# Moving part of a norm phase's vector work to GpSimd, and the order of its start

## The chip, the cores and the metric

One core of a Trainium2 chip runs the whole kernel. The metric is device time in microseconds of one execution; lower is better. Engine names are the profile's: PE is TensorE (with PEld, its weight loads), DVE is VectorE, ACT is ScalarE, POOL is GpSimd, and SP issues most of the DMAs.

## The reference, cut to what matters

The program is one hybrid layer (attention and an mLSTM, both gated) on 256 tokens of width 1024, all float32. The change touches only its first phase: the modulated norm, and the projection of the normed tokens to queries and keys.

```python
ada = c @ w_ada + b_ada
shift, scale, gate = jnp.split(ada[:, None, :], 3, axis=-1)
h = _rmsnorm(x, norm_w) * (1 + scale) + shift
(qa, ka, va, za, qm, km, vm, zm, om, ig, fg, ga, gm) = jnp.split(h @ w_in, SPLIT_IDX, axis=-1)
```

`qa` and `ka` are the first 2048 columns of `h @ w_in`. Everything behind (the other projections, attention, mLSTM, output) is the same program text before and after.

## The kernel before, in words

Every product of the layer keeps close to float32 accuracy by splitting each operand into a high part (rounded to the matmul's format) and a low part (what is left), and adding three products: high by high, high by low, low by high. `hTh` and `hTl` are the two parts of the normed tokens, transposed; `wrh` and `wrl` are those of the weight rows of this phase.

The norm phase runs over eight contraction blocks k of 128 rows of `w_in`. In one block the kernel needs:

- two reductions over the row blocks of `w_ada` (tile `adat`) against the broadcast `c` (tile `cb`), which give the scale column `Ab` and the shift column `Bb` (`modulation` for block 0, `modulation_sum` behind, on DVE; the accumulator is read out by a second short instruction);
- `hTh` and `hf`, x's transposed block times `Ab` plus `Bb`, on ACT, and `hTl = hf - hTh` on DVE (`modulate`, `modulate_low`);
- the high part of 2048 weight columns by casts on ACT (`split_hi`), the low part by subtractions on DVE (`split_low`, line 192);
- 24 matmuls of 128x512 on PE (`mm_row`, line 202) into four accumulators `pm[0..3]`, one for each 512 columns.

Before block 0 x's sums of squares are taken, a power gives the reciprocal norm (`rstd`, on POOL), ACT scales an identity by it (`diag`), and PE multiplies x's blocks by that diagonal: this transposes and norms them at once (`x_transposes`, tile `xps`); copies bring the result from PSUM to `xnT`.

No scheduler decides the order: the engines take their instructions in the order in which the program text issues them. That order is written by hand in the string `P1_STEPS`. Each step is a letter and a block: `i`/`j` are hTh and hf, `U`, `z` the low parts of the first and second 512 columns, `v` that of the last 1024 (`g` and `h` are its halves), `G` is hTl, `c` and `k` the scale and shift reductions, `a` and `b` what ACT makes of them, `w`, `x`, `y` the high parts, `e` the block's matmuls, `R` the copies that lay out the relative bias (on POOL), `L` the next loads. `P1_LOADS` is the order of the DMAs on SP: `Ak1`/`Ak0` are the scale and shift rows of block k (512 KB each), `Wkp` the pieces of its weight rows. Behind the norm phase the next products begin with lines 1178 to 1180 (matmuls) and 519 (their weights' low parts).

Of the kernel before, what the change touches and what calls it, by code (L numbers as in the profile page):

```python
# [70 lines left out]
def tile_hybrid(ctx: ExitStack, tc: tile.TileContext, x, c, params2, w_row, w_va, ada_mod, ada_gate,  # L71
                w_in, w_att_proj, w_ml_proj, w_out, out):
    nc = tc.nc
# [67 lines left out]
    def load_row(k, piece):
        if k not in wrow:
            wrow[k] = rawp.tile([128, 2048], F32, name="raw", tag=f"raw{k % 6}", bufs=1)
        cs = slice(*W_PIECES[piece])
        nc.sync.dma_start(wrow[k][:, cs], w_row[k, :, cs])

    def modulation(k):

        kc = slice(k, k + 1)
        for s, m, b, r in ((1, prm[:, P_NW + k:P_NW + k + 1], b1[:, kc], Ab), (0, 1.0, prm[:, P_SH + k:P_SH + k + 1], Bb)):  # L150
            nc.vector.tensor_tensor_reduce(sq, adat[k][:, s], cb, m, b, OP.mult, OP.add, r[:, kc])
# [16 lines left out]
    def modulate(k, parts="ij"):  # L168
        kc = slice(k, k + 1)
        src = xnT[:, k] if k else xps[0][:, 0]  # L170
        if "i" in parts:
            nc.scalar.activation(hTh[:, k], src, AF.Identity, scale=Ab[:, kc], bias=Bb[:, kc])
# [3 lines left out]
        if k:
            nc.scalar.activation(hf[k], src, AF.Identity, scale=Ab[:, kc], bias=Bb[:, kc])
        else:
            nc.vector.tensor_scalar(hf[k], src, Ab[:, kc], Bb[:, kc], op0=OP.mult, op1=OP.add)

    def modulate_low(k):
        nc.vector.tensor_tensor(hTl[:, k], hf[k], hTh[:, k].bitcast(F32), op=OP.subtract)
# [1 line left out]
    def split_hi(k, c0, c1, copy=nc.scalar.copy):  # L184
        if k not in wsp:
            wsp[k] = (ph.tile([128, NR], F32R, name="wrh", bufs=3), ph.tile([128, NR], F32R, name="wrl", bufs=3))
        copy(wsp[k][0][:, c0:c1], wrow[k][:, c0:c1])  # L187

    def split_low(k, e, c0, c1):
        h, l = wsp[k]  # L190
        cs = slice(c0, c1)
        e.tensor_tensor(l[:, cs], wrow[k][:, cs], h[:, cs].bitcast(F32), op=OP.subtract)  # L192
# [24 lines left out]
    ssa = ph.tile([128, 8], F32, name="ssa")[:, 0:1]  # L217
    cb = ph.tile([128, D], F32, name="cb")

    def rstd(t):  # L220
        nc.gpsimd.tensor_tensor(rsx[:, t:t + 1], ssx[:, t:t + 1], mhalf[:, 0:1], op=OP.pow)


# [19 lines left out]
    nc.vector.tensor_tensor_reduce(sq, xt[:, 0], xt[:, 0], 1.0 / D, EPS, OP.mult, OP.add, ssx[:, 0:1])  # L243
    rstd(0)
    nc.scalar.activation(xnT[:, 4:6].rearrange("p k s -> p (k s)"), xt[:, 1, 0:512], AF.Square, scale=1.0 / 32, accum_out=ssa)
    nc.vector.tensor_tensor_reduce(sq[:, 512:D], xt[:, 1, 512:D], xt[:, 1, 512:D], 1.0 / D, EPS, OP.mult, OP.add, ssx[:, 1:2])
    nc.vector.tensor_tensor(ssx[:, 1:2], ssx[:, 1:2], ssa, op=OP.add)
# [77 lines left out]

# [929 lines left out]
```

## Time and profile before

| | before |
|---|---|
| median of 3 runs | 346.5 us (346.23 to 347.0) |
| the profiled execution | 346.51 us, span 344.5 us |
| busy in the span: PE, DVE, ACT, POOL | 339.0, 276.6, 228.7, 85.7 us |
| PE's clock as granted | 0.998 of full speed |
| HBM read over the span | 82.43 MB |

The page gives busy times by engine, a map of the span in 40 slices, the chain of work that ended last, and groups of instructions by line; the trace behind it gives each instruction's start and duration. A timeline row reads: start, duration, engine, line, operation, written tile <- read tiles, shapes, how many were merged into the row, and in brackets how long the engine had been idle and what it waited for. An instruction's duration can overlap its follower's by some 0.1 us, so what one costs in a row of many is read from start to start.

### The profile page before, as it was taken

To read this page: it belongs to the slowest core of one execution; us is meant where nothing else is said; L and a number is where in the kernel's file an instruction comes from. 1 tells how busy PE (TensorE), PEld (TensorE's weight loads), DVE (VectorE), ACT (ScalarE), POOL (GpSimd) and SP (SyncE) were. 2 spreads that over 40 slices of the span, in tenths; PEclk is the share of its full clock that TensorE was granted. 3 is DMA by queue.
4 is the path that set the end of the run, shared out by engine and by line. 5 is a ranking of instruction groups with operands and counts; after the bars stand their busy time and mean duration, and the time that the engine had idled before them with its cause. 6 is when DMAs were issued, how large, how long until landed. Compare 5 with 4: busy or idle time off the path is not lost.

```text
span 344.5 us, 6230 instructions
## 1 busy us (share of the span) xinstructions
PE 339.0 (98%) x2408; PEld 318.2 (92%) x2408; DVE 276.6 (80%) x420; ACT 228.7 (66%) x355; POOL 85.7 (25%) x83
## 2 busy tenths in 40 slices
PE   7999999999999999999999999999999999999996
PEld 7787889999999999999998888888989999999995
DVE  6999996979995979776997878897797677769952
ACT  4868779799787676766757577777666563735410
POOL 4700002843201836554131233422000102000000
PEclk9999999999999999999999999999999999999999
DMA  7999999989581496267797999999998038260011
GB/s 300 417 412 416 415 419 421 314 287 359 153 338 62 163 380 242 84 209 272 254 280 199 191 180 256 255 240 276 351 357 337 1 124 331 98 245 0 2 61 63
DMA packets 30909, 84.09 MB, mean 244 GB/s; under 512 B 3224, under 2 KB 5152, under 8 KB 30240
## 3 DMA queue, kind: packets, MB, share of 16 engines
q1 hardware_dynamic: 26376, 74.78, 57.8%
q0 software_dynamic: 4352, 8.39, 14.0%
...
q14 instruction: 10, 0.08, 0.1%
HBM read 82.43 MB, written 1.25 MB: 243 GB/s over the span
## 4 chain that ended last, share of the span: by engine, by line
PE 98%; ACT 1%; POOL 0%; DVE 0%; issue 0%; POOLq 0%
PE mm L1188 15%; PE mm L1185 15%; PE mm L1187 15%; PE pm L202 13%; PE mm L1178 4%; PE mm L1180 4%; PE mm L1179 4%; PE aux L1161 4%; PE aux L1162 4%; PE aux L1163 4%; PE mm L1171 3%; PE xps L267 1%; PE mm L1200 1%; PE aux L709 1%; PE mm L1199 1%; PE mm L1198 1%
## 5 line engine op out<-in xcount | busy, mean ns | idle before, releaser
L519 DVE TENSOR_TENSOR wl<-raw,wh 128x1024 fp32r<-128x1024 f32 (+1 forms) x104 | 126.3, 1228 | 34.3 <-ACT wh L515 33.4
L515 ACT CAST wh<-raw 128x1024 fp32r<-128x1024 f32 (+1 forms) x112 | 111.7, 1018 | 24.5 <-PE mm L1187 11.7
L1185 PE MATMUL mm<-hTh,wh 128*128 128x256 f32 x320 | 90.0, 281 | 0.0
L1187 PE MATMUL mm<-hTl,wh 128*128 128x256 f32 x320 | 88.8, 278 | 0.0
L1188 PE MATMUL mm<-hTh,wl 128*128 128x256 f32 x320 | 88.8, 278 | 0.0
L1187 PEld LDWEIGHTS mm<-hTl,wh 128*128 128x128 f32 x320 | 60.3, 189 | 0.2
L1185 PEld LDWEIGHTS mm<-hTh,wh 128*128 128x128 f32 x320 | 60.2, 188 | 0.2
L1188 PEld LDWEIGHTS mm<-hTh,wl 128*128 128x128 f32 x320 | 60.2, 188 | 0.0
L768 POOL DMA_DIRECT2D raw<-in_w_in_dram x16 | 19.5, 1222 | 49.3 <-DVE wl L519 38.3
L1178 PE MATMUL mm<-wh,hTh 128*128 128x344 f32 (+1 forms) x80 | 28.0, 350 | 0.0
L1180 PE MATMUL mm<-wh,hTl 128*128 128x344 f32 (+1 forms) x80 | 27.7, 346 | 0.0
L1179 PE MATMUL mm<-wl,hTh 128*128 128x344 f32 (+1 forms) x80 | 27.7, 346 | 0.0
L519 POOL TENSOR_TENSOR wl<-raw,wh 128x1024 fp32r<-128x1024 f32 x8 | 20.0, 2531 | 15.8 <-ACT wh L515 10.5
L187 ACT CAST wrh<-raw 128x512 fp32r<-128x512 f32 (+1 forms) x24 | 18.2, 761 | 7.6 <-DMA raw<-in_w_row_dram 7.6
L192 DVE TENSOR_TENSOR wrl<-raw,wrh 128x512 fp32r<-128x512 f32 (+1 forms) x26 | 20.5, 811 | 1.1 <-ACT wrh L187 1.1
L202 PE MATMUL pm<-wrh,hTh 128*128 128x512 f32 x64 | 19.8, 391 | 0.0
L202 PE MATMUL pm<-wrh,hTl 128*128 128x512 f32 x64 | 19.8, 391 | 0.0
L202 PE MATMUL pm<-wrl,hTh 128*128 128x512 f32 x64 | 19.1, 396 | 0.0
L1188 PE MATMUL mm<-yah,wl 128*128 128x256 f32 x64 | 17.7, 276 | 0.0
L1185 PE MATMUL mm<-ymh,wh 128*128 128x256 f32 x64 | 17.7, 276 | 0.0
L1185 PE MATMUL mm<-yah,wh 128*128 128x256 f32 x64 | 17.7, 276 | 0.0
L1187 PE MATMUL mm<-yal,wh 128*128 128x256 f32 x64 | 17.7, 276 | 0.0
(252 smaller groups left out, 774.0 us busy)
## 6 DMA issues: line engine op xcount, KB each, us to landing
...
```

The lines of the kernel that those rows point to most:

```text
L187: copy(wsp[k][0][:, c0:c1], wrow[k][:, c0:c1])
L192: e.tensor_tensor(l[:, cs], wrow[k][:, cs], h[:, cs].bitcast(F32), op=OP.subtract)
L202: nc.tensor.matmul(pm[ch][:, t], a[:, k, t * 128:(t + 1) * 128], b[:, cs], start=k == 0 and i == 0, stop=k == KT - 1 and i == 2)
L515: nc.scalar.copy(h, w)
L519: e.tensor_tensor(l, w, h.bitcast(F32), op=OP.subtract)
L768: nc.gpsimd.dma_start(rawt[li][:, ks], w_block(ch["name"], *BLOCK_SUMS[ch["product"]])[:, ks], accum_op=OP.add)
L1178: nc.tensor.matmul(o, a, wh[:, kk], start=first, stop=False)
L1179: nc.tensor.matmul(o, a, wl[:, kk], start=False, stop=False)
L1180: nc.tensor.matmul(o, b, wh[:, kk], start=False, stop=last)
L1185: nc.tensor.matmul(o, wh[:, kk, cs], sh_[:, k], start=first and i % 2 == 0, stop=False, skip_group_check=True)
L1187: nc.tensor.matmul(o, wh[:, kk, cs], sl_[:, k], start=False, stop=False, skip_group_check=True)
L1188: nc.tensor.matmul(o, wl[:, kk, cs], sh_[:, k], start=False, stop=last and i % 2 == 1, skip_group_check=True)
```

## The change: what it does

1. In every block the low part of the last 512 columns (1536 to 2047) is subtracted on POOL and no longer on DVE; DVE keeps 1024 to 1535. In block 0 both of these are on POOL, and so is one cast.
2. The statistics of x: the first tile is squared and summed in halves on DVE and ACT, the second wholly on ACT; POOL scales the first diagonal, ACT the second. The copies that bring `cb` from PSUM go from ACT to DVE.
3. Block 0's two modulation sums are taken in halves of 512, each half with its own DMA.
4. All transposes of x's first tile come ahead of those of the second. In block 0, hf goes from DVE to ACT, the first cast and the first copy of `xnT` from ACT to DVE.
5. Block 1's last weight piece is loaded ahead of block 2's scale rows. The relative-bias copies move from block 0 to the ends of blocks 1 and 2.

The core of the diff:

```diff
-P1_LOADS = ["A01 A00 W00 W01 A11 A10"] + [f"W{k}0 W{k}2 A{k + 1}1 W{k}3 A{k + 1}0" for k in range(1, 7)] + ["W70 W72 W73"]
+P1_LOADS = (["a01 b01 a00 b00 W00 W02 W03 A11 A10", "W10 W12 W13 A21 A20"]
+            + [f"W{k}0 W{k}2 A{k + 1}1 W{k}3 A{k + 1}0" for k in range(2, 7)] + ["W70 W72 W73"])
...
+        half = ph.tile([128, 2], F32, name="sums", bufs=2)
         for s, m, b, r in (...):
-            nc.vector.tensor_tensor_reduce(sq, adat[k][:, s], cb, m, b, OP.mult, OP.add, r[:, kc])
+            for cs, init, to in ((slice(0, D // 2), b, half[:, s:s + 1]), (slice(D // 2, D), half[:, s:s + 1], r[:, kc])):
+                nc.vector.tensor_tensor_reduce(sq[:, cs], adat[k][:, s, cs], cb[:, cs], m, init, OP.mult, OP.add, to)
...
+        if t:
+            nc.gpsimd.tensor_scalar(ssx[:, 1:2], ssa[:, 1:2], 1.0, EPS, op0=OP.mult, op1=OP.add)
+        else:
+            nc.vector.tensor_tensor(ssx[:, 0:1], ssx[:, 0:1], ssa[:, 0:1], op=OP.add)
         nc.gpsimd.tensor_tensor(rsx[:, t:t + 1], ssx[:, t:t + 1], mhalf[:, 0:1], op=OP.pow)
...
+    xsq = xnT[:, 4:8].rearrange("p k s -> p (k s)")
+    nc.vector.tensor_tensor_reduce(sq[:, 0:512], xt[:, 0, 0:512], xt[:, 0, 0:512], 1.0 / D, EPS, OP.mult, OP.add, ssx[:, 0:1])
+    nc.scalar.activation(xsq[:, 0:512], xt[:, 0, 512:D], AF.Square, scale=1.0 / 32, accum_out=ssa[:, 0:1])
+    rstd(0)
+    nc.gpsimd.tensor_scalar(diag[:, 0], ident, rsx[:, 0:1], None, op0=OP.mult)
     for n in range(2):
-        nc.scalar.copy(cb[:, n * 512:(n + 1) * 512], pc[:, n])
+        nc.vector.tensor_copy(cb[:, n * 512:(n + 1) * 512], pc[:, n])
+    nc.scalar.activation(xsq, xt[:, 1], AF.Square, scale=1.0 / 32, accum_out=ssa[:, 1:2])
     rstd(1)
+    nc.scalar.activation(diag[:, 1], ident, AF.Copy, scale=rsx[:, 1:2])
...
+                 w=lambda k: split_hi(k, 0, 512, nc.scalar.copy if k else nc.vector.tensor_copy), ...
+                 g=lambda k: split_low(k, nc.vector, 1024, 1536),
+                 h=lambda k: split_low(k, nc.gpsimd, 1536, NR), p=lambda k: split_low(k, nc.gpsimd, 1024, 1536),
+                 Y=lambda k: split_hi(k, 1024, 1536), Z=lambda k: split_hi(k, 1536, NR, nc.gpsimd.tensor_copy),
```

`P1_STEPS` is a table of steps, so its effect is shown as the order in which the engines then have their instructions. First DVE from block 3's hTl to block 4's, before (`adat`, `cb` are read by the reductions, called ISA here; `wrl` is a low part):

```order
L182 TENSOR_TENSOR hTl<-hf,hTh 128x256
L158 ISA sq,sums<-adat,cb 128x1024
L158 ISA sums 128x1
L192 TENSOR_TENSOR wrl<-raw,wrh 128x512
L158 ISA sq,sums<-adat,cb 128x1024
L158 ISA sums 128x1
L192 TENSOR_TENSOR wrl<-raw,wrh 128x1024
L192 TENSOR_TENSOR wrl<-raw,wrh 128x512
L182 TENSOR_TENSOR hTl<-hf,hTh 128x256
```

The same place of DVE in the changed program:

```order
L182 TENSOR_TENSOR hTl<-hf,hTh 128x256
L161 ISA sq,sums<-adat,cb 128x1024
L161 ISA sums 128x1
L192 TENSOR_TENSOR wrl<-raw,wrh 128x512
L161 ISA sq,sums<-adat,cb 128x1024
L161 ISA sums 128x1
L192 TENSOR_TENSOR wrl<-raw,wrh 128x512 x2
L182 TENSOR_TENSOR hTl<-hf,hTh 128x256
```

The subtraction of 1024 columns behind the second reduction has become one of 512; the order is otherwise the same.

POOL from the powers of the statistics on, before (`rvec` is the relative bias):

```order
L221 TENSOR_TENSOR rsx<-ssx,mhalf 128x1 x2
L291 COPY rvec<-xt 128x16
L296 COPY rvec<-xt 128x3
L296 COPY rvec<-xt 128x2
L296 COPY rvec<-xt 128x3 x2
```

POOL from the same place on, in the changed program, up to block 2's subtraction:

```order
L228 TENSOR_TENSOR rsx<-ssx,mhalf 128x1
L252 TENSOR_SCALAR diag<-ident,rsx 128x128
L225 TENSOR_SCALAR ssx<-ssa 128x1
L228 TENSOR_TENSOR rsx<-ssx,mhalf 128x1
L187 CAST wrh<-raw 128x512
L192 TENSOR_TENSOR wrl<-raw,wrh 128x512 x3
L299 COPY rvec<-xt 128x16
L304 COPY rvec<-xt 128x3
L304 COPY rvec<-xt 128x2
L304 COPY rvec<-xt 128x3 x2
L304 COPY rvec<-xt 128x4 x2
L304 COPY rvec<-xt 128x5
```

A scaling, a cast and three subtractions (two of block 0, one of block 1) now stand ahead of the bias copies, of which nine come before block 2's subtraction and eight before block 3's; those of blocks 4 to 7 follow with nothing between them.

More of the change, by code (lines that the diff above doesn't have):

```diff
@@ L35 @@
 P_CB, P_CW, P_ML, P_QN, P_KN, P_G, P_GT, NPRM2 = 0, 16, 80, 88, 89, 90, 91, 99
-P1_LOADS = ["A01 A00 W00 W01 A11 A10"] + [f"W{k}0 W{k}2 A{k + 1}1 W{k}3 A{k + 1}0" for k in range(1, 7)] + ["W70 W72 W73"]
-P1_STEPS = ("K5 D0 D1 D2 E0 E1 E2 T3 C0 w0 R0 R1 R2 R3 U0 H0 G0 x0 t0 B0 P0 z0 y0 t3 B2 t2 t1 B1 c1 a1 w1 k1 g0 h0 Q0 q0 n0 m0 "
+P1_LOADS = (["a01 b01 a00 b00 W00 W02 W03 A11 A10", "W10 W12 W13 A21 A20"]
+            + [f"W{k}0 W{k}2 A{k + 1}1 W{k}3 A{k + 1}0" for k in range(2, 7)] + ["W70 W72 W73"])
+P1_STEPS = ("K5 D0 D1 D2 D3 E0 E1 E2 E3 C0 H0 w0 U0 G0 t0 x0 B0 P0 z0 Z0 t3 Y0 B2 t1 t2 B1 p0 h0 c1 a1 w1 k1 Q0 q0 N0 M0 "
             + "".join(f"b{k} i{k} U{k} j{k} G{k} x{k} L1 c{k + 1} z{k} y{k} a{k + 1} "
-                      f"w{k + 1} " + (f"g{k} k{k + 1} h{k}" if k == 2 else f"k{k + 1} v{k}") + f" e{k} " for k in range(1, 7))
-            + "b7 i7 U7 j7 G7 x7 z7 y7 v7 P7 Q7 q7 N7 M7").split()
+                      f"w{k + 1} k{k + 1} g{k} h{k} {('R0 R1', 'R2 R3')[k - 1] if k < 3 else ''} e{k} " for k in range(1, 7))
+            + "b7 i7 U7 j7 G7 x7 z7 y7 g7 h7 P7 Q7 q7 N7 M7").split()
 WARM = 5
@@ L134, in tile_hybrid, with load_ada @@
     adat, wrow, wsp, hf = {}, {}, {}, {}
-    def load_ada(k, h):
+    def load_ada(k, h, c0=0, c1=D):
         if k not in adat:
             adat[k] = ph.tile([128, 2, D], F32, name="adat", bufs=4)
-        nc.sync.dma_start(adat[k][:, h], ada_mod[k, h])
+        nc.sync.dma_start(adat[k][:, h, c0:c1], ada_mod[k, h, :, c0:c1])
     def load_row(k, piece):
@@ L175, in modulate @@
         hf[k] = ph.tile([128, S], F32, name="hf", bufs=2)
[L176 to L179, printed above, removed]
+        nc.scalar.activation(hf[k], src, AF.Identity, scale=Ab[:, kc], bias=Bb[:, kc])
     def modulate_low(k):
@@ L210, in next_loads @@
             for what, k, p in P1_LOADS[lp[0]].split():
-                (load_ada if what == "A" else load_row)(int(k), int(p))
+                if what == "W":
+                    load_row(int(k), int(p))
+                else:
+                    load_ada(int(k), int(p), *dict(A=(0, D), a=(0, D // 2), b=(D // 2, D))[what])
             lp[0] += 1
@@ L216, in tile_hybrid @@
     sq = ph.tile([128, D + 632], F32, name="sq")[:, 0:D]
-    ssa = ph.tile([128, 8], F32, name="ssa")[:, 0:1]
+    ssa = ph.tile([128, 8], F32, name="ssa")[:, 0:2]
     cb = ph.tile([128, D], F32, name="cb")
     def rstd(t):
+        if t:
+            nc.gpsimd.tensor_scalar(ssx[:, 1:2], ssa[:, 1:2], 1.0, EPS, op0=OP.mult, op1=OP.add)
+        else:
+            nc.vector.tensor_tensor(ssx[:, 0:1], ssx[:, 0:1], ssa[:, 0:1], op=OP.add)
         nc.gpsimd.tensor_tensor(rsx[:, t:t + 1], ssx[:, t:t + 1], mhalf[:, 0:1], op=OP.pow)
@@ L240, in tile_hybrid @@
                          start=q == 0, stop=q == 1, skip_group_check=True)
-    for n in range(2):
-        nc.scalar.copy(cb[:, n * 512:(n + 1) * 512], pc[:, n])
[L243 to L247, printed above, removed]
+    xsq = xnT[:, 4:8].rearrange("p k s -> p (k s)")
[3 more added lines that the diff above has]
+    nc.gpsimd.tensor_scalar(diag[:, 0], ident, rsx[:, 0:1], None, op0=OP.mult)
+    for n in range(2):
+        nc.vector.tensor_copy(cb[:, n * 512:(n + 1) * 512], pc[:, n])
+    nc.scalar.activation(xsq, xt[:, 1], AF.Square, scale=1.0 / 32, accum_out=ssa[:, 1:2])
     rstd(1)
-    for t in range(2):
-        nc.scalar.activation(diag[:, t], ident, AF.Copy, scale=rsx[:, t:t + 1])
+    nc.scalar.activation(diag[:, 1], ident, AF.Copy, scale=rsx[:, 1:2])
     nc.vector.scalar_tensor_tensor(b1, prm[:, P_SC:P_SC + 8], 1.0, prm[:, P_NW:P_NW + 8], op0=OP.add, op1=OP.mult)
@@ L271, in x_copy @@
         k0 = 0 if kp else 1
-        nc.scalar.copy(xnT[:, 2 * kp + k0:2 * kp + 2, :], xps[kp][:, k0:2])
+        copy = (nc.vector.tensor_copy, nc.scalar.copy, nc.scalar.copy, nc.scalar.copy)[kp]
+        copy(xnT[:, 2 * kp + k0:2 * kp + 2, :], xps[kp][:, k0:2])
     pm = [None, None, None, None]
@@ L313, in tile_hybrid @@
                  D=lambda k: x_transposes(k, (0,)), E=lambda k: x_transposes(k, (1,)),
-                 w=lambda k: split_hi(k, 0, 512), x=lambda k: split_hi(k, 512, 1024), y=lambda k: split_hi(k, 1024, NR),
+                 w=lambda k: split_hi(k, 0, 512, nc.scalar.copy if k else nc.vector.tensor_copy), x=lambda k: split_hi(k, 512, 1024), y=lambda k: split_hi(k, 1024, NR),
                  U=lambda k: split_low(k, nc.vector, 0, 512), z=lambda k: split_low(k, nc.vector, 512, 1024),
-                 v=lambda k: split_low(k, nc.vector, 1024, NR), g=lambda k: split_low(k, nc.vector, 1024, 1536),
-                 h=lambda k: split_low(k, nc.vector, 1536, NR), G=modulate_low,
+                 g=lambda k: split_low(k, nc.vector, 1024, 1536),
+                 h=lambda k: split_low(k, nc.gpsimd, 1536, NR), p=lambda k: split_low(k, nc.gpsimd, 1024, 1536),
+                 Y=lambda k: split_hi(k, 1024, 1536), Z=lambda k: split_hi(k, 1536, NR, nc.gpsimd.tensor_copy), G=modulate_low,
                  c=lambda k: modulation_sum(k, 1), k=lambda k: modulation_sum(k, 0),
```

1 line of the change is left out of this document (removed).

## The prediction

> **What bounds the kernel now.** First the head of the page and the chain that ended last.
>
> ```profile
> span 344.5 us, 6230 instructions
> PE 339.0 (98%) x2408; PEld 318.2 (92%) x2408; DVE 276.6 (80%) x420; ACT 228.7 (66%) x355; POOL 85.7 (25%) x83
> ...
> PE 98%; ACT 1%; POOL 0%; DVE 0%; issue 0%; POOLq 0%
> ...
> 6.93 3.84 PE xps L267 x32
> ```
>
> PE is busy for 98% of the span, and 98% of the chain is PE (the third line), from the transposes at 6.93 us on. A matmul that starts later than before therefore moves the end by as much, and so does one that starts earlier. Call the eight contraction blocks of the norm phase 0 to 7, and T0 to T7 the start of each block's first matmul. The profile cut at these times, with the wait view of PE's weight loads:
>
> ```profile
> 10.53:16.59 6.06, 6.06 (x28) 4.38 (x26) 5.86 (x11) 5.79 (x12) 4.89 (x13) 1.00 1.03 416
> 27.51:33.30 5.79, 5.78 (x26) 4.35 (x24) 5.54 (x10) 4.69 (x9) 0.00 (x0) 1.00 1.03 410
> 33.30:38.76 5.46, 5.46 (x25) 4.50 (x24) 5.46 (x9) 4.32 (x8) 0.00 (x0) 1.00 1.04 416
> 49.64:55.08 5.44, 5.44 (x25) 4.50 (x24) 3.74 (x5) 4.54 (x6) 0.00 (x0) 1.00 1.02 419
> ...
> PEld pm L202 <- DVE wrl L192: 1.3, 4, 0.4
> ```
>
> After stretch and length the columns are PE, PEld, DVE, ACT, POOL, clock, DMA share, GB/s. An undisturbed block is 5.44 us of PE. Blocks 0 and 3 take 6.06 and 5.79, so 0.62 and 0.35 are lost to late low parts. That is the whole stock of waits here: about 1.0 us. DVE has no free time in block 4 (5.46 of 5.46), and POOL does nothing after block 0. So DVE is the second bound, and one block of it has to be read instruction by instruction, with ACT's part at its end:
>
> ```profile
> 32.73 0.42 DVE L182 TENSOR_TENSOR hTl<-hf,hTh 128x256 fp32r<-128x256 f32 x1
> 33.06 1.22 DVE L158 CUSTOM_DVE_ANT_0 sq<-adat,cb 128x1024 f32<-128x1024 f32 x1
> 34.21 0.68 DVE L192 TENSOR_TENSOR wrl<-raw,wrh 128x512 fp32r<-128x512 f32 x1
> 34.81 1.22 DVE L158 CUSTOM_DVE_ANT_0 sq<-adat,cb 128x1024 f32<-128x1024 f32 x1
> 35.96 1.82 DVE L192 TENSOR_TENSOR wrl<-raw,wrh 128x1024 fp32r<-128x1024 f32 x2
> 36.91 0.59 ACT L177 ACTIVATE hf<-xnT,Bb,Ab 128x256 f32<-128x256 f32 x1
> 37.70 0.42 DVE L182 TENSOR_TENSOR hTl<-hf,hTh 128x256 fp32r<-128x256 f32 x1
> ```
>
> hTl to hTl is 37.70 - 32.73 = 4.97 us, 0.47 less than PE's 5.44. That surplus lets DVE run ahead, and it is why blocks 4 to 7 have no wait.
>
> **The repeated part of the change.** In each block the last 512 columns' low part goes from DVE to POOL. DVE loses half of a 128x1024 subtraction. The double row at 35.96 lasts 1.74 us to the hTl, so the 1024 takes 1.74 - 0.60 = 1.14 and the 512 takes 0.60: 0.54 saved. The new order is reduction, 512, 512, hTl. Block 2 of before already has it:
>
> ```profile
> 25.04 1.22 DVE L158 CUSTOM_DVE_ANT_0 sq<-adat,cb 128x1024 f32<-128x1024 f32 x1
> 26.18 1.29 DVE L192 TENSOR_TENSOR wrl<-raw,wrh 128x512 fp32r<-128x512 f32 x2
> 27.75 0.43 DVE L182 TENSOR_TENSOR hTl<-hf,hTh 128x256 fp32r<-128x256 f32 x1 [0.28 <-ACT hf L177]
> ```
>
> There hTl waited 0.28 us for ACT: after the shift reduction come Bb, hTh and hf on ACT, and two short subtractions don't cover them. So half of the 0.54 turns into a new wait. The DVE loop is 0.33 (hTl) + 1.15 + 0.60 (rows at 32.73 to 34.81) + 2.71 (25.04 to 27.75) = 4.79, if POOL costs DVE nothing. These rows tell whether it does:
>
> ```profile
> 123.74 1.31 POOL L717 TENSOR_TENSOR yal<-yf,yah 128x512 fp32r<-128x512 f32 x1 [4.02 <-ACT yah L716]
> 126.66 1.27 DVE L980 CUSTOM_DVE_ANT_0 raw<-raw,cbg,prm 128x1024 f32<-128x1024 f32 x1
> 127.47 1.63 POOL L717 TENSOR_TENSOR yal<-yf,yah 128x512 fp32r<-128x512 f32 x1 [2.42 <-ACT yah L716]
> 127.86 2.32 DVE L980 CUSTOM_DVE_ANT_0 raw<-raw,cbg,prm 128x1024 f32<-128x1024 f32 x1
> 129.06 3.39 POOL L519 TENSOR_TENSOR wl<-raw,wh 128x1024 fp32r<-128x1024 f32 x1
> 130.23 2.43 DVE L749 SCALAR_TENSOR_TENSOR qmT<-mm,prm,qmT 128x255 f32<-128x255 f32 x6
> ...
> 110.93 1.62 POOL L717 TENSOR_TENSOR yal<-yf,yah 128x512 fp32r<-128x512 f32 x1 [19.29 <-ACT yah L716]
> 111.83 1.80 DVE L519 TENSOR_TENSOR wl<-raw,wh 128x1024 fp32r<-128x1024 f32 x1 [0.44 <-ACT wh L515]
> ```
>
> A POOL subtraction of 128x512 takes 1.31 us alone. The one at 127.47 started under a DVE reduction that ended at 127.93, and ended 1.17 after that. The next DVE reduction took 2.32 instead of 1.27 and ended 1.08 after POOL's end (129.10). The subtraction at 111.83 (1.80 instead of 1.14 + 0.08) ended 1.08 after POOL's end (112.55) too. The two engines take turns, whole instructions at a time, when DVE reads two operands from SBUF; the six that read PSUM (130.23) kept 0.4 us each under a POOL operation. All of DVE's subtractions and reductions in the norm phase read two SBUF operands. So one POOL subtraction costs DVE 2.32 - 1.27 = 1.05, and the loop becomes 4.79 + 1.05 = 5.84, 0.40 above PE's 5.44. Bounds for the 1.05: 0.58 (the 1.80 row, where DVE came 0.9 late into POOL's turn) and 1.31 (POOL's whole duration). The Trainium skill (SBUF — State Buffer, Who interferes with whom) has the rule that speaks against this edit: of a DVE instruction with two SBUF inputs and a GpSimd one that reads SBUF, whoever issues first has the shared ports for the whole instruction and the other "fully blocks". The trace agrees on the turns, though what DVE pays is 1.05, not 1.31; by the rule's letter the loop would be 6.10 and the total of this part 5 x 0.26 = 1.3 us more. I take 1.05, the only row with DVE queued back to back as here.
>
> **Blocks 0 and 1.** More of the start moves:
>
> ```profile
> 4.49 1.23 DVE L243 CUSTOM_DVE_ANT_0 sq<-xt 128x1024 f32<-128x1024 f32 x1 [1.49 <-DMA xt<-in_x_dram]
> 5.87 0.57 POOL L221 TENSOR_TENSOR rsx<-ssx,mhalf 128x1 f32<-128x1 f32 x1 [3.66 <-DVE ssx L243]
> 5.88 0.72 DVE L246 CUSTOM_DVE_ANT_0 sq<-xt 128x512 f32<-128x512 f32 x1 [0.16 <-DMA xt<-in_x_dram]
> 9.73 0.08 DVE L151 DVE_READ_ACCUMULATOR2_ANT Bb<- 128x1 f32 x1
> 9.91 0.56 ACT L172 ACTIVATE hTh<-xps,Bb,Ab 128x256 fp32r<-128x256 f32 x1 [0.34 <-DVE Bb L151]
> 12.03 1.22 DVE L158 CUSTOM_DVE_ANT_0 sq<-adat,cb 128x1024 f32<-128x1024 f32 x1
> 13.42 1.23 DVE L158 CUSTOM_DVE_ANT_0 sq<-adat,cb 128x1024 f32<-128x1024 f32 x1 [0.16 <-DMA adat<-in_ada_mod_dram]
> 16.82 1.21 DVE L158 CUSTOM_DVE_ANT_0 sq<-adat,cb 128x1024 f32<-128x1024 f32 x1
> 17.10 1.05 ACT L187 CAST wrh<-raw 128x1024 fp32r<-128x1024 f32 x1 [0.41 <-DMA raw<-in_w_row_dram]
> ...
> 109.51 0.68 DVE L715 TENSOR_TENSOR yf<-aux,zat 128x512 f32<-128x512 f32 x1
> ```
>
> x's first half lands at 4.5. Half sums (0.72) on two engines, a short add (0.1 to 0.3 with its waits) and the power (0.57) give 6.0; POOL's scaling of the identity shows in no row, so 0.1 to 0.6 (the read at 9.73 and the power): the first transposes at about 6.5, not 6.93. The second tile's squares on ACT (1024 from 5.9 on, 1.05 to 1.23 by the cast at 17.10 and the reduction) and three small operations of up to 0.57 each come at about 8.5; 16 transposes of 0.12 (32 in 3.84) then end by 10.4. DVE meanwhile copies cb out of PSUM (two times 0.60 to 0.68 by the 109.51 row), from 5.5 to 6.8, and then sums block 0 in four halves of 0.72: Bb at about 9.7 against 9.81. hTh follows at +0.1, 0.56 long, so T0 is 10.4 against 10.53. DVE's first cast (at most the 0.68 of a 512 subtraction) and low part lie beside hTh and PE's first two matmuls, hf on ACT beside them too; without that cover PE would wait for hTl up to the 0.35 that block 3 lost. I enter 0, bounds -0.2 and +0.3.
>
> Block 0's low parts 3 and 4 go to POOL, where p0 can start once ACT has cast its columns (hTh, hf, a cast, a copy and that cast, about 0.5 each from 9.8: 12.4). DVE's next reduction has started by then (12.03). By turns: reduction to 13.3, p0 to 14.5, reduction (data at 13.3) to 15.6, h0 to 16.7, then DVE's first low part of block 1 (0.55), hTl 0.33, and the reduction for block 2 at 17.6, not 16.82. PE needs h0 for its last two matmuls of block 0: 16.75 + 0.11 + 2 x 0.23 gives T1 = 17.4 against 16.59: **+0.8**. Bounds: 10.4 + 5.45 = 15.9 if POOL is free (-0.7), and 17.9 if p0 gets its turn before the reduction (+1.3).
>
> The loads: block 1's last weight piece goes ahead of block 2's scale rows. The cast at 17.10 waited for that piece; the scale rows, now second of the two, land then instead. That is hidden by DVE, which isn't there until 17.6; with that cover gone the reduction would start at 17.2, still 0.4 late. The extra DMA issues on SP (nine in place of six ahead of block 1) cost nothing: the DMA share stays at 1.03 in all these stretches. The relative-bias copies go from POOL's start into blocks 1 and 2, behind and ahead of its subtractions; they are read only by a DMA behind all these loads, so being later costs nothing by itself; what stands behind them is a rival below.
>
> **The sum.** Block 2's reduction starts at 17.6. Five loops of 5.84 put block 7's at 46.8. From there block 6's rest, 1.15 + 0.60 + 1.05 + 1.15 + 0.68 = 4.63, then four matmuls with one wait (0.06 + 0.11 + 0.91): T7 = 52.5, against 49.64. So T1 to T7 is 35.1, against 33.05: **+2.05**. Bounds: +0.3 if the 0.28 wait and some of the hold overlap (loop 5.49), and +3.4 at 6.10. Block 7 is 5.44 as before, 0: its POOL part is due 5.0 after T7. Behind it:
>
> ```profile
> 50.07 1.65 DVE L519 TENSOR_TENSOR wl<-raw,wh 128x688 fp32r<-128x688 f32 x2
> 55.23 0.32 PE L1179 MATMUL mm<-wl,hTh 128*128 128x344 f32 x1
> ```
>
> The next phase's first low part was ready 4.3 us early (50.94 against 55.23). DVE now comes to it at about 55.7 and ends it at 56.6; PE wants it at 58.1. Still covered by 1.5: 0. In all 0 + 0.8 + 2.05 = +2.85. The profiled execution took 346.51 us (span 344.5), 0.01 above the median of 346.5: **349.4 us**.
>
> **Rivals.** (1) Faster: POOL's turns fall where DVE waits or reads PSUM, so that DVE pays under 5.44 - 4.79 = 0.65 a block. Then PE never waits: the 0.62 and 0.35 of waits go and T0 comes 0.1 early, 345.4. The 2.43 row speaks for it; against it, no DVE instruction of the loop but the wait of 0.28 leaves room. (2) No change: DVE pays about 0.65 to 0.8 and the late T1 is bought back by waits that go, 346.5. (3) POOL's own queue jams. It had:
>
> ```profile
> 8.48 6.94 POOL L296 COPY rvec<-xt 128x3 f32<-128x3 f32 x16
> ```
>
> 16 copies in 6.94 us, when DVE was often idle. Nine now stand ahead of block 2's subtraction and eight ahead of block 3's. If each waits for one DVE instruction of about 0.9, that is 8 and 7 us where a loop leaves 5.84 - 1.2: block 3's part comes 2.8 late, 352.2. Speaking against: copies pass several at a time in any wait of DVE.
>
> **Chances.** A difference under 0.2% (0.7 us) can't be told from none. The forecast 0.68 (its own range 348.0 to 351.2), jam 0.11, no change 0.08, faster 0.13: slower 0.79. The range 346.0 to 352.3 leaves out the faster case and a tail.
>
> **What would show it.** Right: DVE reductions of about 2.3 us next to each POOL subtraction; hTl waiting some 0.3 for hf; the loop near 5.8; T1 near 17.4, phase end near 58; nothing changed behind. Wrong: reductions that stay at 1.22 under POOL, or a loop under 5.44.

## The result and the profile after

The changed kernel takes 351.36 us in the median of four runs (350.79 to 351.52), against 346.6 us for the kernel before, measured beside it: a ratio of 1.0132, 95% interval 1.0120 to 1.0144. It is slower by 4.8 us; the prediction was 2.9. The profiled execution took 350.79 us, the shortest of the four.

The page of the changed kernel, its span, its busy times and the chain that ended last:

```profile
span 348.7 us, 6252 instructions
PE 341.1 (98%) x2408; PEld 318.5 (91%) x2408; DVE 282.4 (81%) x422; ACT 226.9 (65%) x353; POOL 105.1 (30%) x95
...
PE 84%; DVE 4%; DMA 4%; issue 3%; ACT 2%; SPq 1%; DVEq 0%
```

POOL is busy 19 us longer, yet DVE, from which work was taken, is busy 6 us longer too. The chain that was 98% PE is now 84% PE; in the norm phase it runs through DVE, ACT and the loads as well. The same phase cut at the first matmuls of its blocks (blocks 0, 1, 3, 4 and 7 of the changed kernel; columns as in the prediction's stretches), and the waits of PE's weight loads in the phase:

```profile
10.72:17.92 7.20, 6.21 (x27) 4.39 (x25) 6.91 (x10) 5.59 (x12) 5.19 (x3) 1.00 1.03 416
17.92:24.40 6.48, 5.78 (x26) 4.43 (x25) 6.20 (x10) 4.16 (x9) 5.25 (x10) 1.00 1.03 411
29.89:35.77 5.88, 5.78 (x26) 4.43 (x24) 5.60 (x9) 3.62 (x8) 3.10 (x3) 1.00 1.03 415
35.77:41.67 5.90, 5.77 (x25) 4.43 (x24) 5.61 (x9) 3.74 (x8) 1.76 (x1) 1.00 1.03 418
53.49:58.99 5.50, 5.50 (x26) 4.51 (x24) 5.16 (x7) 5.50 (x8) 1.89 (x2) 1.00 0.86 314
...
PEld pm L202 <- DVE wrl L192: 3.4, 5, 1.1
PEld pm L202 <- POOL wrl L192: 1.8, 2, 1.0
```

The last two rows read: total wait in us, number of waits, the longest. Waits for low parts that were 1.3 us in all (on DVE's) are now 5.2, and they stand in blocks 4 to 6 too, where there were none. Block 0 is 1.14 longer, a block of the loop 0.46. The loop of DVE from hTl to hTl, and POOL's subtraction beside it:

```profile
35.57 0.43 DVE L182 TENSOR_TENSOR hTl<-hf,hTh 128x256 fp32r<-128x256 f32 x1 [0.28 <-ACT hf L179]
35.91 1.22 DVE L161 CUSTOM_DVE_ANT_0 sq<-adat,cb 128x1024 f32<-128x1024 f32 x1
...
37.05 0.69 DVE L192 TENSOR_TENSOR wrl<-raw,wrh 128x512 fp32r<-128x512 f32 x1
37.66 2.32 DVE L161 CUSTOM_DVE_ANT_0 sq<-adat,cb 128x1024 f32<-128x1024 f32 x1
...
39.91 1.28 DVE L192 TENSOR_TENSOR wrl<-raw,wrh 128x512 fp32r<-128x512 f32 x2
41.48 0.43 DVE L182 TENSOR_TENSOR hTl<-hf,hTh 128x256 fp32r<-128x256 f32 x1 [0.29 <-ACT hf L179]
...
37.13 1.76 POOL L192 TENSOR_TENSOR wrl<-raw,wrh 128x512 fp32r<-128x512 f32 x1 [4.14 <-DVE sums L161]
```

POOL's subtraction starts at 37.13 under DVE's, waits for it, and ends at 38.89; the reduction started at 37.66 and ends 1.09 after that. It took 2.32 where its neighbour took 1.22. DVE lost 0.54 us of work and got 1.10 of waiting, and 0.28 more for hf.

The totals of all kernels beside the places in the phase, each from its profile:

| kernel | block 0 begins | block 1 | block 7 | phase ends | profiled us | median, ratio to before |
|---|---|---|---|---|---|---|
| before | 10.53 | 16.59 | 49.64 | 55.08 | 346.51 | 346.6 |
| changed | 10.72 | 17.92 | 53.49 | 58.99 | 350.79 | 351.36, 1.0132 |
| e2_only_the_loop | 11.35 | 17.31 | 52.84 | 58.29 | 349.64 | 350.18, 1.0097 |
| e1_low_on_dve | 10.81 | 18.43 | 53.10 | 58.59 | 350.04 | 348.51, 1.0048 |
| e3_memset | 11.02 | 18.65 | 52.14 | 57.63 | 348.94 | 348.02, 1.0053 |
| e4_start_alone | 10.86 | 17.35 | 50.76 | 56.25 | 347.49 | 347.97, 1.0031 |
| e5_256_columns | 10.80 | 17.77 | 51.31 | 56.80 | 348.37 | 350.44, 1.0081 |
| e6_g0_first | 10.58 | 16.29 | 49.68 | 55.12 | 346.54 | 346.69, 1.0003 |
| e7_old_load_order | 10.72 | 17.16 | 50.77 | 56.26 | 348.00 | 347.63, 1.0024 |
| e8_before_moved | 10.54 | 16.61 | 49.78 | 55.27 | 346.83 | 346.92, 1.0005 |
| e9_after_moved | 10.59 | 18.21 | 53.82 | 59.27 | 350.71 | 350.71, 1.0116 |
| before_again | 10.79 | 16.84 | 49.80 | 55.24 | 346.66 | 346.66 |
| after_again | 10.87 | 18.20 | 53.81 | 59.30 | 350.75 | 350.75 |

The kernel before beside them took 347.13 (e1 to e4), 346.64 (e5 to e7) and 346.74 us (e8, e9, after_again). The ratios are those on record, with their intervals, and are not quotients of two medians: for e5 the medians would give 1.011. A start of block 0 repeats to 0.26 us between two profiles of one kernel.

### The profile page after: what moved, and what is told of

It reads as the page before. It is cut to its first block, busy times and chain, and to the rows that moved or that the text cites. A ratio compares the mean times of both kernels' runs of the same rounds, so it can differ in the third digit from the quotient of the medians.

```text
span 348.7 us, 6252 instructions
## 1 busy us (share of the span) xinstructions
PE 341.1 (98%) x2408; PEld 318.5 (91%) x2408; DVE 282.4 (81%) x422; ACT 226.9 (65%) x353; POOL 105.1 (30%) x95
## 4 chain that ended last, share of the span: by engine, by line
PE 84%; DVE 4%; DMA 4%; issue 3%; ACT 2%; SPq 1%; DVEq 0%
PE mm L1193 15%; PE mm L1196 15%; PE mm L1195 15%; DMA raw<-in_w_row_dram 4%; PE mm L1188 4%; PE mm L1186 4%; PE mm L1187 4%; DVE sq L161 4%; PE aux L1169 4%; PE aux L1170 4%; PE aux L1171 4%; PE mm L1179 3%; PE pm L202 2%; PE aux L717 1%; PE mm L1206 1%
## 5 line engine op out<-in xcount | busy, mean ns | idle before, releaser
L161 DVE CUSTOM_DVE_ANT_0 sq<-adat,cb 128x1024 f32<-128x1024 f32 x14 | 23.4, 1670 | 0.2 <-DMA adat<-in_ada_mod_dram 0.2
L192 POOL TENSOR_TENSOR wrl<-raw,wrh 128x512 fp32r<-128x512 f32 x9 | 16.3, 1819 | 19.1 <-ACT wrh L187 10.8
L202 PEld LDWEIGHTS pm<-wrl,hTh 128*128 128x128 f32 x64 | 11.5, 188 | 7.3 <-DVE wrl L192 3.4
L192 DVE TENSOR_TENSOR wrl<-raw,wrh 128x512 fp32r<-128x512 f32 x23 | 17.7, 788 | 0.4 <-ACT wrh L187 0.3
L1195 PE MATMUL mm<-yml,wh 128*128 128x256 f32 x64 | 17.7, 276 | 0.0
```

The lines of the kernel that those rows point to most:

```text
L161: nc.vector.tensor_tensor_reduce(sq, adat[k][:, s], cb, 1.0, 0.0, OP.mult, OP.add, sums[k][:, s:s + 1])
L202: nc.tensor.matmul(pm[ch][:, t], a[:, k, t * 128:(t + 1) * 128], b[:, cs], start=k == 0 and i == 0, stop=k == KT - 1 and i == 2)
L1195: nc.tensor.matmul(o, wh[:, kk, cs], sl_[:, k], start=False, stop=False, skip_group_check=True)
```

## The experiments

**e1: the loop's low part back on DVE, the rest of the change kept.**

```diff
-                 h=lambda k: split_low(k, nc.gpsimd, 1536, NR),
+                 h=lambda k: split_low(k, nc.vector if k else nc.gpsimd, 1536, NR),
```

> The changed kernel with one part undone: in blocks 1 to 7 the low part of the last 512 columns is subtracted on DVE again (start and block 0 stay as changed). Turns (each POOL subtraction costs DVE about 1.1 us): the loop goes from 5.91 to 0.34 + 1.14 + 0.60 + 1.15 + three times 0.60 = 5.0 us of DVE, below PE's 5.45 to 5.5, so T1 stays near 17.9, the phase ends near 56.3, and the time is about 348.6 (2.0 above before, 2.8 below the changed kernel). Rival start (the loss is made in the first two blocks): no more than 0.5 below the changed kernel, 350.9. Rival pace (the matmuls run at 0.230 instead of 0.227 us each): the same as the changed kernel.

Measured 348.51 us, ratio 1.0048 (1.0026 to 1.0070). The loop of DVE is 5.04 (hTl at 29.10, 34.14 and 39.18), as expected, and PE waits for nothing from block 2 on. So taking POOL out of blocks 1 to 7 gives back about 2.9 us of the 4.6 that the ratios show (1.0132 less 1.0048). The rest belongs to the start, with block 0's part on POOL. The times of e1 spread from 347.4 to 350.0; its profile shows why one was long. Its stretches before and after block 1's first matmul (18.43), and block 2:

```profile
15.40:18.80 3.40, 1.85 (x8) 0.90 (x7) 2.62 (x3) 2.03 (x6) 3.40 (x10) 1.00 1.02 413
18.90:22.30 3.40, 3.40 (x10) 2.63 (x9) 3.39 (x7) 2.36 (x5) 3.40 (x7) 0.50 1.04 424
25.63:31.13 5.50, 5.50 (x26) 4.51 (x24) 5.50 (x10) 4.19 (x9) 0.00 (x0) 1.00 1.03 415
```

PE waited for block 1's hTh, was busy for 1.85 of 3.40 us, and the next 3.41 us were granted half the clock, which is 1.7 us lost. The granted clocks of all runs fit this: e1's two long runs (350.04 and 349.84) have 0.995 and 0.993, the other five 1.0. Without these two the median is 347.70, 0.57 above the kernel before, so POOL's part of the loop is worth more than the 2.9 us, and the start less than 1.38.

**e2: the loop's low part on POOL, the start as before.**

```diff
-                      f"w{k + 1} " + (f"g{k} k{k + 1} h{k}" if k == 2 else f"k{k + 1} v{k}") + f" e{k} " for k in range(1, 7))
+                      f"w{k + 1} " + f"k{k + 1} g{k} h{k} e{k} " for k in range(1, 7))
-                 h=lambda k: split_low(k, nc.vector, 1536, NR), G=modulate_low,
+                 h=lambda k: split_low(k, nc.gpsimd if k else nc.vector, 1536, NR), G=modulate_low,
```

> The kernel before with one part of the change alone: in blocks 1 to 7 the last 512 columns' low part on POOL, in the changed order of steps; start, block 0, loads and bias copies as before. Turns: T1 stays at 16.6, the reductions of block 2 begin at 16.8 and the loop is 5.9 long, so T7 is near 52.1 instead of 49.6: 2.5 above before, 349.1. Rival start: no change, 346.6. If turns cost DVE only its own share of the ports (a slower rate, no blocking), the loop stays under 5.44: 346.3.

Measured 350.18, ratio 1.0097 (1.0083 to 1.0112). The same rows in this kernel, which has the old start and no bias copies in its loop:

```profile
34.92 0.43 DVE L182 TENSOR_TENSOR hTl<-hf,hTh 128x256 fp32r<-128x256 f32 x1 [0.29 <-ACT hf L177]
...
37.01 2.32 DVE L158 CUSTOM_DVE_ANT_0 sq<-adat,cb 128x1024 f32<-128x1024 f32 x1
...
40.83 0.42 DVE L182 TENSOR_TENSOR hTl<-hf,hTh 128x256 fp32r<-128x256 f32 x1 [0.28 <-ACT hf L177]
...
36.48 1.76 POOL L192 TENSOR_TENSOR wrl<-raw,wrh 128x512 fp32r<-128x512 f32 x1 [4.14 <-DVE sums L158]
```

The loop is 5.91, the reduction 2.32, as in the changed kernel. This one part of the change, alone, costs 3.05 us between the medians. This profile's loads came 0.8 later than before's, so its places are read as differences. Block 1 to block 7 takes 35.53 us, against 33.05. From block 0's start to the phase's end the kernel before takes 44.55 us, e2 2.39 more, e1 1.53 more (without the 1.7 of its clock), and the changed kernel 3.72 more: the two parts add up to within 0.2 us. In the medians they do so less well: e2's 3.05 with e1's 1.38 is 4.43 of 4.76 us, but with 0.57 (e1 at full clock) it is 3.62.

**e3: POOL busy at the same places, but writing only.** Blocks 1 to 7 leave out the low part of the last 512 columns; POOL writes zeros there, twice, in its place.

```diff
-                 h=lambda k: split_low(k, nc.gpsimd, 1536, NR),
+                 h=lambda k: [nc.gpsimd.memset(wsp[k][1][:, 1536:NR].bitcast(F32), 0.0) for _ in range(2)] if k
+                     else split_low(k, nc.gpsimd, 1536, NR),
```

> The changed kernel with POOL's subtraction of blocks 1 to 7 replaced by two POOL memsets of the same 512 columns, each 0.5 to 0.6 us (0.42 for 384 columns before), together as long as one subtraction; that low part is left out. POOL is as busy and writes as much, but reads nothing from SBUF. Turns for reading: DVE's reductions stay at 1.22, the loop is 4.8, PE's 5.45 is the bound, about 348.4. Turns for any POOL instruction: DVE loses two times 0.5, reductions of 1.7 and more, the loop is 5.8 and the time is that of the changed kernel or 0.3 below it, 351.1.

Measured 348.02, ratio 1.0053 (1.0029 to 1.0077), near e1's time. (Its two long runs, 350.01 and 350.59, were granted 0.995 of the clock, as in e1.) A reduction, the next hTl, and the POOL writes beside the reduction:

```profile
35.80 1.23 DVE L161 CUSTOM_DVE_ANT_0 sq<-adat,cb 128x1024 f32<-128x1024 f32 x1
...
38.52 0.43 DVE L182 TENSOR_TENSOR hTl<-hf,hTh 128x256 fp32r<-128x256 f32 x1 [0.28 <-ACT hf L179]
...
35.88 1.11 POOL L325 MEMSET wrl<- 128x512 f32 x2 [4.38 <-DVE wrl L192]
```

POOL ran for 1.11 us under the reduction, and neither was held up: 1.23, and two writes of 0.55. So it isn't POOL's being busy that holds DVE, nor its writing into SBUF; what is left of the subtraction is its reading from SBUF, or the subtracting itself, which no run separates. POOL's bias copies, which read but subtract nothing, wait for DVE too: in the kernel before, one of two columns ran from 8.61 to 9.85, to 0.05 us behind the end of the reduction at 8.52, where those of four columns took 0.18. The Trainium skill (SBUF — State Buffer, Who interferes with whom) says just this: a DVE instruction with two SBUF inputs contends with a GpSimd one that reads SBUF, not with one that only writes it. The rows of e2 and e3 agree.

**e5: POOL takes 256 columns instead of 512.**

```diff
-                 g=lambda k: split_low(k, nc.vector, 1024, 1536),
-                 h=lambda k: split_low(k, nc.gpsimd, 1536, NR),
+                 g=lambda k: split_low(k, nc.vector, 1024, 1792),
+                 h=lambda k: split_low(k, nc.gpsimd, 1792 if k else 1536, NR),
```

> The changed kernel with POOL's part of blocks 1 to 7 cut from 512 columns to 256 (DVE subtracts 768 columns instead of 512 in each block). Turns, whole instructions at a time: POOL's instruction is about half as long (0.65 to 0.85 us), what DVE pays is about 0.45 to 0.6 in place of 1.10, and DVE's own part grows by about 0.25, so the loop is 5.91 - 0.55 + 0.25 = 5.6 or a little less, 0.1 above PE's 5.5 at most: block waits nearly gone, total about 349.0 (348.3 to 349.8), between the changed kernel (351.4) and the one with the low part on DVE alone (348.5). A fixed price of a meeting, whatever the length of POOL's instruction: DVE pays 1.1 still, the loop is 6.15, total 353.

One loop in the profile:

```profile
39.06 0.43 DVE L182 TENSOR_TENSOR hTl<-hf,hTh 128x256 fp32r<-128x256 f32 x1
...
41.15 1.77 DVE L161 CUSTOM_DVE_ANT_0 sq<-adat,cb 128x1024 f32<-128x1024 f32 x1
...
44.42 0.43 DVE L182 TENSOR_TENSOR hTl<-hf,hTh 128x256 fp32r<-128x256 f32 x1
...
40.62 1.21 POOL L192 TENSOR_TENSOR wrl<-raw,wrh 128x256 fp32r<-128x256 f32 x1 [4.75 <-DVE sums L161]
```

The hold is 1.77 - 1.22 = 0.55, half of 1.10 for half the columns: DVE pays by the length of POOL's instruction, not a fixed price for a meeting. (Where it doesn't wait, POOL's subtraction takes 0.75 us for 256 columns and 1.31 for 512; DVE pays 0.2 less each time.) The loop is 5.36, under PE's 5.50, and from block 4 on nothing waits. The profiled run took 348.37. The median, 350.44 (ratio 1.0081, 1.0054 to 1.0107), missed the expectation: of five runs two took 348.4 and 348.6, three 350.4 to 350.7, and those three have no profile. A clock step like e1's, of 1.7 us, can be the cause in one of the three at most: 350.44 was granted 0.995 of the clock, but 350.66 and 350.68 were granted 1.0. What made those two long stays open. So e5 shows what one meeting costs DVE; that a loop under PE's 5.50 also brings the time down it shows in two runs of five.

**e4: the start and its loads alone.** Statistics in halves, block 0's sums in halves, the transposes' order and all loads as in the change; every low part as before.

```diff
-P1_STEPS = ("K5 D0 D1 D2 D3 E0 E1 E2 E3 C0 H0 w0 U0 G0 t0 x0 B0 P0 z0 Z0 t3 Y0 B2 t1 t2 B1 p0 h0 c1 a1 w1 k1 Q0 q0 N0 M0 "
+P1_STEPS = ("K5 D0 D1 D2 D3 E0 E1 E2 E3 C0 H0 w0 R0 R1 R2 R3 U0 G0 t0 x0 B0 P0 z0 y0 t3 B2 t2 t1 B1 c1 a1 w1 k1 g0 h0 Q0 q0 n0 m0 "
...
-                      f"w{k + 1} k{k + 1} g{k} h{k} {('R0 R1', 'R2 R3')[k - 1] if k < 3 else ''} e{k} " for k in range(1, 7))
+                      f"w{k + 1} " + (f"g{k} k{k + 1} h{k}" if k == 2 else f"k{k + 1} v{k}") + f" e{k} " for k in range(1, 7))
...
-                 h=lambda k: split_low(k, nc.gpsimd, 1536, NR), p=lambda k: split_low(k, nc.gpsimd, 1024, 1536),
+                 h=lambda k: split_low(k, nc.vector, 1536, NR), v=lambda k: split_low(k, nc.vector, 1024, NR),
```

> The changed kernel's start alone: statistics, first diagonal on POOL, halves of block 0's sums, transposes, cb copies, loads as changed; all of the weights' low parts on DVE and high parts on ACT but block 0's first, and the loop and bias copies as before. T0 near 10.7 as in the changed kernel (10.53 before). DVE's reduction for block 1 starts about 0.3 later than before, block 2's at 17.2 because its rows land behind block 1's last weight piece; T1 near 16.9 (16.59 before). Start: 0.3 to 0.6 above before, 347.1. If the halves are worth what they are meant for: 0.3 below before, 346.3.

**e7: e4 with block 1's last weight piece behind block 2's scale rows again.**

```diff
-P1_LOADS = (["a01 b01 a00 b00 W00 W02 W03 A11 A10", "W10 W12 W13 A21 A20"]
+P1_LOADS = (["a01 b01 a00 b00 W00 W02 W03 A11 A10", "W10 W12 A21 W13 A20"]
```

> The kernel with the changed start alone (347.97 against 347.13), but block 1's last weight piece behind block 2's scale rows again, as before the change. If the moved load is what delays block 2's scale reduction (18.06 there) and makes block 1's PE wait 0.42 us, that reduction starts at 17.3 to 17.7, the wait is under 0.15, and the total falls by 0.3 to 0.4, to about 0.45 us above the kernel before. The prediction's step (the load costs nothing, at most 0.4): the upper end. Rival: the wait comes from DVE's own queue or from the cast that now waits for the late weight piece: unchanged, 0.8 above the kernel before.

e4 measured 347.97, ratio 1.0031 (1.0019 to 1.0042); e7 347.63, ratio 1.0024 (1.0012 to 1.0035). Block 2's reduction and blocks 0 and 1 of e4:

```profile
18.06 1.23 DVE L161 CUSTOM_DVE_ANT_0 sq<-adat,cb 128x1024 f32<-128x1024 f32 x1 [0.40 <-DMA adat<-in_ada_mod_dram]
...
10.86:17.35 6.49, 6.05 (x26) 4.37 (x25) 6.08 (x12) 6.09 (x12) 3.57 (x11) 1.00 1.03 418
17.35:23.29 5.94, 5.80 (x25) 4.38 (x24) 5.54 (x10) 3.99 (x8) 0.00 (x0) 1.00 1.03 411
```

Blocks 0, 1 and 2 of e7:

```profile
10.72:17.16 6.44, 6.06 (x26) 4.37 (x25) 6.08 (x12) 6.04 (x12) 3.52 (x11) 1.00 1.03 417
17.16:22.68 5.52, 5.52 (x25) 4.50 (x24) 5.31 (x9) 3.98 (x8) 0.00 (x0) 1.00 1.03 412
22.68:28.46 5.78, 5.78 (x25) 4.35 (x24) 4.88 (x8) 3.12 (x6) 0.00 (x0) 1.00 1.03 413
```

The late load is real: with it DVE waits 0.40 us and block 1 takes 5.94; with the old order that wait is gone and block 1 is 5.52. But then DVE waits 0.72 us for block 3's scale rows (its reduction starts at 23.19), where e4 has no wait, blocks 2 and 3 take 5.78 and 5.83 instead of 5.50, and both phases end at the same time (56.25 and 56.26). The wait moved on to the next block's rows. The start itself costs 0.8 to 1.0 us. Against the kernel before beside it e4 is 0.84 slower, above the 0.3 to 0.6 expected: 0.43 of it is block 0 (6.49 against 6.06), and its later blocks take 5.50 where 5.44 was measured before, which e8 looks into.

**e6: a try for a better kernel.** The kernel before, with g0 ahead of k1 on DVE.

```diff
-t2 t1 B1 c1 a1 w1 k1 g0 h0 Q0 q0 n0 m0 "
+t2 t1 B1 c1 a1 w1 g0 k1 h0 Q0 q0 n0 m0 "
```

> The kernel before with one step moved: block 0's low part of columns 1024 to 1535 (g0) ahead of the second reduction for block 1 (k1) on DVE, so two low parts stand around one reduction in another order. If block 0's wait of 0.62 us comes from g0 and h0 being queued behind two reductions, PE gets g0 1.2 us earlier and waits for h0 alone, or not at all: 346.5 to 347.0, that is 0.1 to 0.6 us less than the kernel before. If h0 is the last wait anyway, k1 + h0 still end at the same time: no change (within 0.1 us).

Measured 346.69, ratio 1.0003 (0.9988 to 1.0017): nothing. Its blocks 0 and 1:

```profile
10.58:16.29 5.71, 5.71 (x26) 4.46 (x25) 5.65 (x10) 5.25 (x11) 5.71 (x13) 1.00 1.04 420
16.29:22.12 5.83, 5.82 (x25) 4.38 (x24) 5.57 (x10) 4.70 (x9) 0.14 (x1) 1.00 1.03 414
```

Block 0's wait is shorter by 0.35 and block 1's longer by as much; the sum is 11.54, against 6.06 + 5.48 = 11.54 before. DVE's queue was full either way. No kernel tried beats the one before.

**e8: the kernel before with its weight rows at other places in SBUF; e9: the changed kernel with them at the old places.** A buffer gets its place when the program first asks for it. The change asks for `sums` earlier, and for hf ahead of the rows, so `wrh` and `wrl` start 2112 bytes per partition later. e8 moves them by that much, e9 moves them back:

```diff
 e8, in the kernel before
     cb = ph.tile([128, D], F32, name="cb")
+    for _ in range(2):
+        ph.tile([128, 2], F32, name="sums", bufs=2)
+        ph.tile([128, S], F32, name="hf", bufs=2)
 e9, in the changed kernel
     cb = ph.tile([128, D], F32, name="cb")
+    for _ in range(3):
+        ph.tile([128, NR], F32R, name="wrh", bufs=3)
+    for _ in range(3):
+        ph.tile([128, NR], F32R, name="wrl", bufs=3)
+    for _ in range(2):
+        ph.tile([128, S], F32, name="hf", bufs=2)
```

> The kernel before with nothing changed but the place of its split weight rows in SBUF: two small buffers (sums, hf) get their place first, so wrh and wrl start 2112 bytes per partition later, where they lie in the changed kernel. In the profiles so far a 512-column matmul of the norm phase takes 0.443 us per 1000 columns in every kernel with the old start (four of four) and 0.447 in every one with the new start (six of six), 5.44 against 5.49 us a block. If the place of the rows sets it: 0.447 here, blocks 4 to 7 at 5.49 to 5.50, total 0.35 to 0.45 above the kernel before. If it comes from the steps of the new start or from which engine writes the rows: 0.443, blocks 5.44, total unchanged.

> The changed kernel with wrh and wrl at the places that they have in the kernel before, and no other change. If the place sets the matmuls' pace: 0.443 us per 1000 columns; blocks 0 and 1, where PE waits for low parts, gain a little, the loop of DVE stays 5.91 (it is the bound there, so blocks 2 to 6 gain nothing), block 7 goes from 5.50 to 5.44: total 0.1 to 0.2 lower than the changed kernel, 351.2. If the slower matmuls of the next phase (0.159 against 0.153 us from 58 to 72 us) come from the same cause, another 0.4 less: 350.8. If the place is not the cause: 0.447 and 351.4.

e8's block 6, undisturbed:

```profile
44.28:49.78 5.50, 5.50 (x26) 4.51 (x24) 5.24 (x8) 4.79 (x10) 0.21 (x1) 1.00 1.04 420
```

e9's block 7:

```profile
53.82:59.27 5.45, 5.45 (x25) 4.51 (x24) 5.11 (x7) 5.45 (x8) 1.90 (x2) 1.00 0.78 278
```

The pace follows the place in both directions: 5.50 in e8 where it was 5.44, 5.45 in e9 where it was 5.50 (0.447 and 0.443 us per 1000 columns, start to start). In time it is near nothing: e8 346.92, ratio 1.0005 (0.9992 to 1.0017), less than the expected 0.35 to 0.45 at its middle; e9 350.71, ratio 1.0116 (1.0101 to 1.0132), no faster than the one run of after_again beside it (350.75). Where PE waits for DVE, a faster matmul only waits longer. Why the place matters was not looked into.

**before_again and after_again: second profiles.**

> The kernel before, unchanged, for a second profile. If the pace of the matmuls (0.443 us per 1000 columns in the norm phase, 0.153 us for a 344-column one from 58 to 70 us) belongs to the kernel and not to the chip or the moment, it reads 0.443 and 0.153 again; if it drifts between profiles by as much as the changed kernel showed (0.447, 0.159), no part of that difference may be put down to the change.

> The changed kernel, unchanged, for a second profile. If its matmul paces belong to it: 0.447 us per 1000 columns in the norm phase and 0.159 us for a 344-column matmul from 58 to 72 us again. If the second one is of the moment (among the kernels with the new start it was seen in three profiles of six), it can read 0.153, with the end 0.4 us earlier; the first should stay in both.

The pace of the norm phase repeated in both (0.443, 0.447). The one behind it did not: the changed kernel's 344-column matmuls took 0.153 us this time, not 0.159, so the 0.37 us that the first profile lost between 59 and 72 us isn't the change's. What the second profile of the changed kernel showed beside that was not expected. Blocks 0 and 3, two DVE instructions, and on POOL the second eight bias copies and the subtractions of blocks 3 and 4:

```profile
10.87:18.20 7.33, 6.01 (x27) 4.35 (x25) 6.79 (x9) 4.43 (x11) 4.14 (x3) 1.00 1.03 417
30.67:36.66 5.99, 5.78 (x25) 4.43 (x24) 5.71 (x9) 3.88 (x8) 5.57 (x7) 1.00 1.03 417
...
34.90 1.42 DVE L182 TENSOR_TENSOR hTl<-hf,hTh 128x256 fp32r<-128x256 f32 x1 [0.28 <-ACT hf L179]
...
37.38 1.77 DVE L192 TENSOR_TENSOR wrl<-raw,wrh 128x512 fp32r<-128x512 f32 x1
...
28.98 5.80 POOL L304 COPY rvec<-xt 128x6 f32<-128x6 f32 x8
34.74 1.29 POOL L192 TENSOR_TENSOR wrl<-raw,wrh 128x512 fp32r<-128x512 f32 x1
36.45 2.15 POOL L192 TENSOR_TENSOR wrl<-raw,wrh 128x512 fp32r<-128x512 f32 x1 [0.42 <-DVE hTl L182]
```

Here the bias copies did hold block 3's subtraction back: it began at 34.74, 3.5 us later than in the first profile (31.26). It then fell on DVE's hTl, which took 1.42 instead of 0.43, and block 4's on a subtraction (1.77 instead of 0.69). The victim changes, the price doesn't: 1.0 to 1.1 us of DVE for each POOL subtraction, and the phase ends at 59.30 instead of 58.99, of which 0.15 was there at block 0's start. e9's profile shows the same jam (block 3's subtraction at 34.76).

## Why the prediction was right, point by point

**The sum.** The direction and the mechanism were forecast, the size only in part: 4.8 us instead of 2.9, and 351.36 lies just above the range that the prediction gave to its own mechanism (348.0 to 351.2). The profiled execution is 4.28 us longer than before's, 1.43 more than the sum of 2.85: T0 0.19, block 0 0.34, T1 to T7 0.47, block 7 0.06, behind it 0.37. The other three runs of the changed kernel are 0.5 to 0.7 us longer than the profiled one and have no profile.

**The turns: right.** The mechanism was forecast with its price, 1.05 us, and its row, about 2.3 us; the rows show 1.10 and 2.32. e2 shows it alone, e3 takes away POOL's reading and with it the price, e5 halves both (in its profile). The 0.28 us wait of hTl for hf, taken from block 2 of before, stands in blocks 2 to 7. The loop is 5.91 where 5.84 was said. The row chosen for the price (DVE queued back to back) was the right one; the bounds of 0.58 and 1.31 were not reached.

**T0: within what can be told.** Entered as 0, with +0.3 as the upper bound; 0.1 to 0.2 later here, with 0.26 between two profiles of before. The earlier transposes (6.5) did not come: POOL's scaling of the diagonal, in no row of before, took 0.61, the upper end of the 0.1 to 0.6 given, and they began at 6.86, against 6.93 before.

**Block 0 to T1: mechanism right, term too small.** The sum's +0.8 put T1 at 17.4; it was 17.92 in one profile, 18.20 in the other. The step that failed is "DVE's next reduction has started by then (12.03)". The start on DVE and POOL in the changed kernel:

```profile
6.85 0.81 DVE L154 CUSTOM_DVE_ANT_0 sq<-adat,cb,b 128x512 f32<-128x512 f32 x1 [0.21 <-DMA adat<-in_ada_mod_dram]
...
9.92 0.42 DVE L187 CAST wrh<-raw 128x512 fp32r<-128x512 f32 x1
...
11.49 0.42 DVE L280 COPY xnT<-xps 128x256 f32<-128x256 f32 x1
...
12.69 1.23 DVE L161 CUSTOM_DVE_ANT_0 sq<-adat,cb 128x1024 f32<-128x1024 f32 x1
...
14.09 2.06 DVE L161 CUSTOM_DVE_ANT_0 sq<-adat,cb 128x1024 f32<-128x1024 f32 x1 [0.16 <-DMA adat<-in_ada_mod_dram]
...
18.10 1.22 DVE L161 CUSTOM_DVE_ANT_0 sq<-adat,cb 128x1024 f32<-128x1024 f32 x1
...
12.71 4.58 POOL L192 TENSOR_TENSOR wrl<-raw,wrh 128x512 fp32r<-128x512 f32 x2 [0.62 <-ACT wrh L187]
```

The time 12.03 was before's own. Its reduction stands behind a longer queue now: the halves of a sum took 0.74 to 0.82, not 0.72, so Bb came at 10.0 and not 9.7; and the cast, which was costed only as hidden from PE, and the copy at 11.49, which the working left out, are two DVE instructions where one (hf) left. The reduction came at 12.69. From there the turns go as worked out, each 0.6 later: reduction to 13.85, POOL to 15.06, reduction to 16.15, POOL to 17.29, T1 17.9. In after_again POOL started 0.09 us ahead of the reduction and T1 was 18.20: the prediction's upper case for this term, 0.3 above the 17.9 it gave. There PE's longest wait was 1.8 us for block 1's hTh on ACT, which the two held reductions made late, and not for h0, on which the sum rested.

**T1 to T7: +2.05 said, +2.52 measured.** Of the 0.47, five loops of 5.92 on average (hTl at 17.76 to hTl at 47.38) instead of 5.84 make 0.4. Block 2's reduction came at 18.10 instead of 17.6, as T1's lateness has it, which is the term above.

**The swapped load: hidden, as said.** In the changed kernel block 2's reduction has no DMA wait (18.10). With the cover gone (e4) it showed as 0.40 us, the size given, though at 18.06 and not at 17.2; e7 shows that undoing it gains nothing.

**Block 7 and behind: nearly right.** Block 7 takes 0.06 more, by the place of the rows (e8, e9), which the prediction did not consider. Nothing behind was late; the 0.37 of the first profile came from slower matmuls and did not come again in after_again.

**The rivals.** Faster needed DVE to pay under 0.65 a block; e5, at 0.55, is on the other side of that point, and there PE did stop waiting from block 4 on, though no run of e5 was faster than the kernel before. The jam of POOL's copies happened in one of two profiles, 3.5 us late, where 2.8 was worked out, and did not have the price given to it: block 3 took 5.99 us, 0.11 more than in the profile without the jam (5.88).
